# S5 in stages between the weight chunks, its parameters on GpSimd, and partition moves by TensorE products, in a hybrid decoder trunk

## The chip, the cores and the metric

The kernel runs on one core of a Trainium2 chip. The core has five engines with queues of their own: TensorE (PE in the profile; PEld is its weight load), VectorE (DVE), ScalarE (ACT), GpSimd (POOL) and SyncE (SP), and DMA queues that SyncE and ScalarE issue. The metric is the device time of one execution in microseconds; less is better.

## The reference, cut to what matters

Two layers (DEPTH = 2) of width 1024 over T = 272 tokens, in float32. A layer projects the normed input once, feeds four token mixers from it, merges them by gates and ends with an MLP of width 4096.

```python
proj = u @ w_in[l]
(rq, rk, rv, rg, s5u, sz, sxbc, sdt, hq, hf, hi, hgate, gates) = jnp.split(proj, split_at, axis=-1)
y_ret = retention_mixer(rq, rk, rv, rg, ret_gn_w[l])
y_s5 = s5_mixer(s5u, ...)
y_ssd = ssd_mixer(sz, sxbc, sdt, ...)
y_hg = hgrn2_mixer(hq, hf, hi, hgate, lb_all[l], hgrn_norm_w[l])
...
mixed = jnp.sum(gate * proj_b, axis=2) @ w_out[l]
h = h + rms_norm(mixed, norm_post_mix[l])
```

The mixer that is rearranged is S5: 32 groups of 16 channels, with 64 complex states each.

```python
mag = jnp.exp(lr * step)
ab_re, ab_im = mag * jnp.cos(li * step), mag * jnp.sin(li * step)
...
bu_re = jnp.einsum('btgj,gpj->btgp', uf, bb_re)      # and bu_im
_, _, xr, xi = lax.associative_scan(combine, (a_re, a_im, bu_re, bu_im), axis=1)
y = einsum(xr, c_re) - einsum(xi, c_im) + d_skip * u
y = jax.nn.gelu(y)
a, gt = jnp.split(y @ glu_w + glu_b, 2, axis=-1)
return a * jax.nn.sigmoid(gt)
```

Retention turns its queries and keys by a rotary embedding: with x1 and x2 the two halves of 32 channels in a head, `[x1*cos - x2*sin, x1*sin + x2*cos]`.

## The kernel before

**Weights.** All weights come as 336 chunks of 128 x 1024 floats in a fixed order (`ORDER`), 168 a layer. `chunk` (L307) loads one by SyncE's queue into one of three buffers (`wst`); ScalarE rounds it to a high half (`whi`, L325, three buffers), VectorE subtracts that for a low half (`wlo`, L327, two buffers). `gemm` (L331) makes of each block of 128 columns three products with one-pass operands: high by high (L344), high by the activation's low half (L345), low by high (L347). A chunk has 24 such products into a bank `g`, of which there are three. Chunks of a layer, numbered from its start: 0 to 11 HGRN's inputs, 12 to 19 SSD's, 20 to 23 S5's input, 24 to 27 HGRN's gate, 28 to 35 merge gates, 36 to 39 SSD's gate, 40 to 43 HGRN's branch, 44 to 51 merge gates, 52 to 59 retention's queries (52, 53), keys and values, 60 to 63 SSD's branch, 64 to 67 retention's gate, 68 to 83 merge gates, 84 to 87 the GLU of S5, 88 to 95 two branches, then the output projection and the MLP. Products that aren't weight chunks (attention, S5, transposes) are in plain float32 and are recorded as two matmuls each.

**Order.** The program is written as one stream; a planner builds each engine's instruction list ahead of time from it, by priority in the order of the text and by a modelled time at which operands are ready. `high_priority(offset)` moves instructions ahead; `issue_after(x)` puts them behind `x` on its engine. Each engine runs its list strictly in that order.

**S5.** `s5_params` (L833) makes, once for both layers, powers, exponentials and tables from three parameter columns; nearly 200 instructions on VectorE, on 128 x 32 elements mostly. Each layer handles its 16 column groups in four batches. `s5_prep` loads the batch's B and C values by ScalarE's queue into `s5a` and makes from them, on VectorE (three outer products of 128 x 512, three instructions each) and on GpSimd (one, and a table of six instructions, L987 to L992), the operands; `kd` and `bt` are its small products on TensorE. `s5_run` multiplies the input (L1109), scans the states with VectorE and GpSimd, and multiplies out (L1143, L1146). `s5_out` applies GELU to two batches and moves 32-partition blocks to other partitions by 16 copies (L1160 VectorE, L1162 ScalarE). All buffers of a batch (`s5a` to `s5g`) exist once. All four batches stand in the text behind `s5_in`; layer 1's first prepare stands in layer 0 behind `ssd_fin`.

**Rotary.** `ret_in` multiplies a 32-partition half by the sine table into the other half's partitions on GpSimd (L1496, four instructions of 32 x 1088), the whole by the cosine table, and adds.

The functions that the change touches, with their line numbers:

Of the kernel before, what the change touches and what calls it, by code (L numbers as in the profile page):

```python
# [13 lines left out]
ALU = mybir.AluOpType  # L14
# [57 lines left out]
for _name, _w in (("ident", 128), ("ones", 128), ("cen", 128), ("m432", 432), ("he", 1), ("ho", 1), ("le", 1), ("lo", 1),  # L72
                  ("rh", 1), ("rl", 1), ("r1", 1)):
    CONSTS[_name] = (_n, _w)
    _n += _w
# [12 lines left out]
AK, WARM = 5, 14  # L88
LH, LO, LU = (2,), (2,), (2,)
# [4 lines left out]
def shape_constants():  # L94
# [10 lines left out]
    put("cen", np.eye(128) - 1.0 / 128)  # L105
    t = np.arange(T)
# [27 lines left out]
    for i in range(2):  # L134
        for q in range(4):
# [3 lines left out]
            for k in range(2):  # L139
# [3 lines left out]
                sgn = 1.0 if q % 2 == 0 else -1.0  # L143
# [90 lines left out]
class Net:  # L234
    def __init__(self, ctx, tc, io, dbg=None):
# [24 lines left out]
        self.hold = {}  # L260

# [71 lines left out]
    def gemm(self, out, w, wk, x, xk, n, start=True, stop=True, after=None, late=False):  # L333
# [72 lines left out]
    def layer(self, l):  # L406
# [45 lines left out]
        s5y = self.s5(l, self.s5_in(l, u_all))  # L452
# [7 lines left out]
        if not last:  # L460

            idle, self.ahead = self.s5_prep(l + 1, 0)
# [7 lines left out]
        s5y = self.glu(l, s5y, (8, 2), sl)  # L470
# [362 lines left out]
    def s5_params(self):  # L833

        nc = self.nc
        v = nc.vector
# [7 lines left out]
        def tt(o, a, b, op):  # L844
            v.tensor_tensor(out=o, in0=a, in1=b, op=op)

        def ts(o, a, s1, op0, s2=None, op1=None):
            if op1 is None:
                v.tensor_scalar(out=o, in0=a, scalar1=s1, scalar2=None, op0=op0)
            else:  # L850
                v.tensor_scalar(out=o, in0=a, scalar1=s1, scalar2=s2, op0=op0, op1=op1)
# [26 lines left out]
        v.scalar_tensor_tensor(out=cs, in0=z, scalar=-0.5, in1=cs, op0=ALU.mult, op1=ALU.add)  # L878
# [5 lines left out]
        v.scalar_tensor_tensor(out=q, in0=q, scalar=-4.0, in1=k, op0=ALU.mult, op1=ALU.add)  # L884
# [23 lines left out]
        v.memset(pw[:, 0, 0], 1.0)  # L908
        v.memset(pw[:, 1, 0], 0.0)
# [13 lines left out]
        cmul(*P(3), *P(2), *P(1))  # L923
        cmul(*P(4), *P(2), *P(2))
# [18 lines left out]
        for s in (2, 1, 0):  # L943
            cmul(c5[:, 0, s], c5[:, 1, s], cR, cI, *P(3 - s))
# [607 lines left out]
```

## Time and profile before

| | us |
|---|---|
| median of 3 runs | 1277.0 (1274.56 to 1277.59) |
| the profiled execution | 1277.68 |
| its span, first to last instruction | 1275.9 |
| TensorE busy | 1216.1 |
| VectorE busy | 893.0 |
| ScalarE busy | 694.2 |
| GpSimd busy | 411.0 |

The profile is of one execution. Busy time of an engine is the union of its instructions' records; matmul records overlap, since a matmul starts while the one before it drains, so a busy TensorE is not one at its peak. The waits view lists idle time of an engine and what released it. A row by stretch gives the stretch in us from the span's start, its length, then the busy us of PE, PEld, DVE, ACT and POOL with their instructions (x), the granted clock, the share of the DMA engines and GB/s. Granted clock is that of TensorE, 1.00 for 2.4 GHz and 0.50 for 1.2 GHz.

### The profile page before, as it was taken

The numbers are of one execution on the slowest core, as the hardware profiler recorded it, in microseconds if no ns is written. First come the engines' busy times: TensorE is split into PE (matmuls) and PEld (weight loads), VectorE is DVE, ScalarE is ACT, GpSimd is POOL, SyncE is SP. The second block draws the span as 40 slices with busy tenths as digits, with TensorE's granted clock in tenths as the row PEclk, the third lists the DMA queues.
The fourth block names the chain that finished last, engine by engine and source line by source line (L and its number), as shares of the span: only waits on it lengthen the run. The fifth ranks groups of instructions, "written<-read, shape, count | busy, mean of one in ns | idle before, by whom it ended". The sixth has DMA issues, their size and how long they took to land.

```text
span 1275.9 us, 24312 instructions
## 1 busy us (share of the span) xinstructions
PE 1216.1 (95%) x9534; PEld 1174.6 (92%) x9534; DVE 893.0 (70%) x1480; ACT 694.2 (54%) x1219; POOL 411.0 (32%) x422
## 2 busy tenths in 40 slices
PE   8999998879999989999989999988999998999997
PEld 7999897879999989999979998987999998999996
DVE  8999989885637675544468995898656487655444
ACT  7446746443745665544455558354647546665442
POOL 2452467668002142200024333575170031322001
PEclk9999999989999989999989999998999998999998
DMA  6423232344354535555434332333444553555552
GB/s 238 160 98 104 101 123 99 108 136 145 135 175 173 176 110 178 173 175 178 170 108 143 126 123 97 123 111 114 146 150 149 184 179 136 169 188 189 182 184 98
DMA packets 53187, 186.69 MB, mean 146 GB/s; under 512 B 6096, under 2 KB 7248, under 8 KB 53072
## 3 DMA queue, kind: packets, MB, share of 16 engines
q1 hardware_dynamic: 50480, 179.40, 41.2%
q10 hardware_dynamic: 2592, 5.74, 1.4%
q8 instruction: 75, 1.23, 0.4%
q14 instruction: 40, 0.33, 0.1%
HBM read 184.06 MB, written 1.05 MB: 145 GB/s over the span
## 4 chain that ended last, share of the span: by engine, by line
PE 76%; DVE 13%; issue 4%; POOL 3%; ACT 2%; DMA 1%; SPq 0%; DVEq 0%; ACTq 0%; POOLq 0%
PE g L347 22%; PE g L344 22%; PE g L345 22%; DVE wlo L327 3%; PE mb L726 1%; PE ma L1263 1%; PE mb L717 1%; POOL S L1496 1%; DVE h L604 1%; DMA s5a<-in_bc 1%; DVE big_npom L601 1%; DVE s5a L1012 1%; ACT whi L325 1%; PE ma L726 1%; PE mb L1109 1%
## 5 line engine op out<-in xcount | busy, mean ns | idle before, releaser
L327 DVE TENSOR_TENSOR wlo<-wst,whi 128x1024 fp32r<-128x1024 f32 x336 | 438.5, 1306 | 259.1 <-PE g L347 220.8
L325 ACT ACTIVATE whi<-wst 128x1024 fp32r<-128x1024 f32 x336 | 355.8, 1060 | 365.3 <-PE g L345 287.6
L347 PE MATMUL g<-xh_u,wlo 128*128 128x272 f32 (+1 forms) x1024 | 299.7, 294 | 16.0 <-DVE wlo L327 15.8
L344 PE MATMUL g<-xh_u,whi 128*128 128x272 f32 (+1 forms) x1024 | 299.5, 293 | 0.6 <-ACT early L1068 0.4
L345 PE MATMUL g<-xl_u,whi 128*128 128x272 f32 (+1 forms) x1024 | 297.8, 291 | 0.0
L344 PE MATMUL g<-S,whi 128*128 128x272 f32 (+1 forms) x832 | 236.0, 288 | 4.6 <-ACT S L541 4.1
L347 PE MATMUL g<-S,wlo 128*128 128x272 f32 (+1 forms) x808 | 230.0, 288 | 1.7 <-DVE wlo L327 1.7
L345 PE MATMUL g<-S,whi 128*128 128x272 f32 (+1 forms) x768 | 220.4, 289 | 2.2 <-DVE S L552 1.9
L347 PEld LDWEIGHTS g<-xh_u,wlo 128*128 128x128 f32 x1024 | 195.7, 192 | 21.0 <-DVE wlo L327 18.2
L344 PEld LDWEIGHTS g<-xh_u,whi 128*128 128x128 f32 x1024 | 196.5, 192 | 2.6 <-ACT early L1068 0.7
L345 PEld LDWEIGHTS g<-xl_u,whi 128*128 128x128 f32 x1024 | 196.5, 192 | 1.5 <-issue 1.2
L344 PEld LDWEIGHTS g<-S,whi 128*128 128x128 f32 x832 | 157.1, 190 | 5.3 <-ACT S L541 4.5
L347 PEld LDWEIGHTS g<-S,wlo 128*128 128x128 f32 x808 | 151.9, 189 | 2.6 <-DVE wlo L327 2.2
L345 PEld LDWEIGHTS g<-S,whi 128*128 128x128 f32 x768 | 145.8, 190 | 4.1 <-DVE S L552 4.0
L345 PE MATMUL g<-xl_npm,whi 128*128 128x272 f32 (+1 forms) x512 | 147.7, 291 | 1.2 <-DVE xl_npm L552 1.2
L344 PE MATMUL g<-xh_npm,whi 128*128 128x272 f32 (+1 forms) x512 | 143.6, 289 | 2.4 <-ACT xh_npm L541 2.4
L347 PE MATMUL g<-xh_npm,wlo 128*128 128x272 f32 (+1 forms) x496 | 140.5, 288 | 0.0
L345 PEld LDWEIGHTS g<-xl_npm,whi 128*128 128x128 f32 x512 | 99.1, 193 | 1.9 <-DVE xl_npm L552 1.7
L344 PEld LDWEIGHTS g<-xh_npm,whi 128*128 128x128 f32 x512 | 96.7, 193 | 2.9 <-ACT xh_npm L541 2.9
L677 POOL TENSOR_TENSOR acc<-acc,tmp 128x272 f32<-128x272 f32 (+1 forms) x48 | 38.9, 828 | 186.0 <-DVE tmp L676 186.0
L347 PEld LDWEIGHTS g<-xh_npm,wlo 128*128 128x128 f32 x496 | 94.2, 192 | 0.2
L507 POOL TENSOR_TENSOR tmp<-tmp 128x272 f32<-128x272 f32 (+1 forms) x64 | 45.7, 714 | 137.3 <-DVE wlo L327 79.5
(377 smaller groups left out, 2184.4 us busy)
## 6 DMA issues: line engine op xcount, KB each, us to landing
wst<-in_w SPq DMA_DIRECT2D x336, 512.0 KB, 3.5
S<-in_rot ACTq DMA_DIRECT2D x4, 544.0 KB, 6.8
s5a<-in_bc ACTq DMA_DIRECT2D x8, 256.0 KB, 3.4
h<-in_h SPq DMA_DIRECT2D x4, 272.0 KB, 5.5
S<-in_ssdc ACTq DMA_DIRECT2D x2, 384.0 KB, 4.4
dtc<-in_ssdc ACTq DMA_DIRECT2D x2, 272.0 KB, 4.7
out<-h SPq DMA_DIRECT2D x2, 256.0 KB, 2.8
S<-in_lvl SPq DMA_DIRECT2D x1, 448.0 KB, 7.2
```

The lines of the kernel that those rows point to most:

```text
L325: a = nc.scalar.activation(hi, st, AF.Copy)
L327: nc.vector.tensor_tensor(out=lo, in0=st, in1=hi.bitcast(F32), op=ALU.subtract)
L344: self.nc.tensor.matmul(out, lhsT=a, rhs=r, start=st, stop=False)
L345: self.nc.tensor.matmul(out, lhsT=a, rhs=s, start=False, stop=False)
L347: end = self.nc.tensor.matmul(out, lhsT=b, rhs=r, start=False, stop=en)
L507: nc.gpsimd.tensor_tensor(out=q, in0=a, in1=a, op=ALU.mult)
L601: e.tensor_tensor(out=mw[:, k], in0=mw[:, k], in1=r, op=ALU.mult)
L604: e.tensor_tensor(out=self.h[:, k, sl], in0=self.h[:, k, sl], in1=mw[:, k], op=ALU.add)
L677: nc.gpsimd.tensor_tensor(out=a, in0=a, in1=t, op=ALU.add)
L717: nc.tensor.matmul(ps[:, c0:c0 + T - q0], lhsT=k[b, 128 * s:128 * s + 128], rhs=q[b, q0:T], start=True, stop=True)
L726: nc.tensor.matmul(out[:, t:T], lhsT=v01[s] if s < 2 else v2, rhs=P[:, p0:p0 + T - t], start=s == 0, stop=s == 2)
L1012: e.tensor_tensor(out=tmp, in0=X[1 - r], in1=F[1], op=ALU.mult)
```

## The change

S5's four batches are cut into four steps each (prepare, products, states, outputs), and `chunk` starts a step when the chunk count reaches the step's place: batch b's steps at chunks 24 + 10 b + 0, 3, 5 and 8 of the layer. Their first matmuls are put behind the last product of the chunk before. `s5_end` finishes ahead of the GLU. `s5_params` runs on GpSimd, where three-operand instructions become two and some complex products are joined. The partition moves of `s5_out` become products with 32 columns of the identity, 32 in a call, two calls a layer; ScalarE copies or splits their banks. Retention's halves are exchanged by a product with a permutation (`swap`), four a layer, followed by a VectorE and two GpSimd instructions each. The prepare of layer 1's first batch stands behind the GLU. The squares of retention are in slot 4 and not 11.

```diff
+S5_AT = (0, 3, 5, 8), 10
...
+    put("swap", np.eye(128)[p ^ 32])
...
     def chunk(self, *want):
         nc = self.nc
         assert ORDER[self.wi] == want, (ORDER[self.wi], want)
+        while self.stages and self.stages[0][0] <= self.wi:
+            self.stages.pop(0)[1]()
...
+        self.last = end
         return end
...
         if l == 0:
             self.s5_params()
-        s5y = self.s5(l, self.s5_in(l, u_all))
+        self.s5(l, self.s5_in(l, u_all))
...
-        if not last:
-
-            idle, self.ahead = self.s5_prep(l + 1, 0)
...
-        s5y = self.glu(l, s5y, (8, 2), sl)
+        assert not self.stages
+        s5y = self.glu(l, self.s5_end(), (8, 2), sl)
+        if not last:
+
+            idle, self.ahead = self.s5_prep(l + 1, 0)
...
         def tt(o, a, b, op):
-            v.tensor_tensor(out=o, in0=a, in1=b, op=op)
+            g.tensor_tensor(out=o, in0=a, in1=b, op=op)
...
-        v.scalar_tensor_tensor(out=r, in0=k, scalar=-PIO2[0], in1=th, op0=ALU.mult, op1=ALU.add)
-        v.scalar_tensor_tensor(out=r, in0=k, scalar=-PIO2[1], in1=r, op0=ALU.mult, op1=ALU.add)
-        v.scalar_tensor_tensor(out=r, in0=k, scalar=-PIO2[2], in1=r, op0=ALU.mult, op1=ALU.add)
+        for i, c in enumerate(PIO2):
+            ts(z, k, -c, ALU.mult)
+            tt(r, z, r if i else th, ALU.add)
...
-        for s in (2, 1, 0):
-            cmul(c5[:, 0, s], c5[:, 1, s], cR, cI, *P(3 - s))
+        sh = [128, 3, DEPTH, 16]
+        d = d4[:, 0:96].rearrange("p (i l q) -> p i l q", i=3, l=DEPTH)
+        cmul(c5[:, 0, 0:3], c5[:, 1, 0:3], *[pw[:, r, 3:0:-1] for r in range(2)],
+             *[x.unsqueeze(1).to_broadcast(sh) for x in (cR, cI)])
...
     def s5(self, l, W):
-        yf = self.slot(6, [128, 4, 68, 4])
+
+        nc = self.nc
+        yf = self.slot(6, [128, 2, 68, 4])
+        Y = self.cmy[:, 2:4].rearrange("p a (q c) -> p (a q) c", q=4)
+        now = {}
+
+        def prep(b):
+            if l and b == 0:
+                now["fs"], now["prep"] = (), self.ahead
+            else:
+                now["fs"], now["prep"] = self.s5_prep(l, b, self.decay if l and b == 1 else self.begin)
+
+        def products(b):
+            for f in now["fs"]:
+                f(self.tc.issue_after(self.last.ins))
+
+        def states(b):
+            now["run"] = self.s5_run(l, b, W, now["prep"], Y[:, 4 * (b % 2):4 * (b % 2) + 4])
+            next(now["run"])
+
+        def outputs(b):
+            next(now["run"])
+            if b == 1:
+                for i, ps in enumerate(self.s5_out(Y)):
+                    nc.scalar.activation(yf[:, i], ps, AF.Copy)
+
+        def end():
+            gh, gl = self.slot(9, [128, 4, T], F32R), self.slot(7, [128, 4, T], F32R)
+            cs = lambda a: a.rearrange("p (c s) -> p c s", s=4)
+            for i in range(2):
+                self.split(yf[:, i], cs(gh[:, i]), cs(gl[:, i]))
+            for i, ps in enumerate(self.s5_out(Y)):
+                self.split(ps, cs(gh[:, 2 + i]), cs(gl[:, 2 + i]))
+            return gh, gl
+
+        self.s5_end = end
         for b in range(4):
...
+            for at, f in zip(S5_AT[0], (prep, products, states, outputs)):
+                self.stages.append((self.wi + b * S5_AT[1] + at, lambda f=f, b=b: f(b)))
...
-        for q in range(4):
+        out = []
+        for a in range(2):
+            ps = self.bank("mb")[:, :T].rearrange("p (s c) -> p s c", s=4)
             for s in range(4):
-                o, i = yf[32 * q:32 * q + 32, b:b + 2, :, s], G[32 * s:32 * s + 32, :, q, :]
-                if q % 2:
-                    nc.vector.tensor_copy(o, i)
-                else:
-                    nc.scalar.activation(o, i, AF.Copy)
+                for q in range(4):
+                    nc.tensor.matmul(ps[32 * q:32 * q + 32, s], lhsT=self.c("ident")[:, 32 * s:32 * s + 32],
+                                     rhs=G[:, a, q], start=True, stop=True)
+            out.append(ps.rearrange("p s c -> p c s"))
+        return out
...
-        for q in range(4):
-            a, b = slice(32 * q, 32 * q + 32), slice(32 * (q ^ 1), 32 * (q ^ 1) + 32)
-            g.tensor_tensor(out=sw[b], in0=qk[a], in1=rot[1][a], op=ALU.mult)
-        g.tensor_tensor(out=qk, in0=qk, in1=rot[0], op=ALU.mult)
         qf, k = self.slot(14, [128, 4, T]), self.kpad[1]
         q = qf[:, 0:2]
-        g.tensor_tensor(out=q, in0=qk[:, 0:2], in1=sw[:, 0:2], op=ALU.add)
-        g.tensor_tensor(out=k[:, :, 0:T], in0=qk[:, 2:4], in1=sw[:, 2:4], op=ALU.add)
+        for i in range(4):
+
+            ps = self.bank()[:, :T]
+            nc.tensor.matmul(ps, lhsT=self.c("swap"), rhs=qk[:, i], start=True, stop=True)
+            nc.vector.tensor_tensor(out=sw[:, i], in0=ps, in1=rot[1][:, i], op=ALU.mult)
+            g.tensor_tensor(out=qk[:, i], in0=qk[:, i], in1=rot[0][:, i], op=ALU.mult)
+            g.tensor_tensor(out=q[:, i] if i < 2 else k[:, i - 2, 0:T], in0=qk[:, i], in1=sw[:, i], op=ALU.add)
...
-        sq, r = self.slot(11, [128, 4, T]), self.slot(1, [128, 4, T])
+        sq, r = self.slot(4, [128, 4, T]), self.slot(1, [128, 4, T])
```

## Rows read from the trace of the kernel before

**Rows 1.** The page: busy time of each engine, and a group of products

```profile
...
PE 1216.1 (95%) x9534; PEld 1174.6 (92%) x9534; DVE 893.0 (70%) x1480; ACT 694.2 (54%) x1219; POOL 411.0 (32%) x422
...
L347 PE MATMUL g<-xh_u,wlo 128*128 128x272 f32 (+1 forms) x1024 | 299.7, 294 | 16.0 <-DVE wlo L327 15.8
...
```

**Rows 2.** Busy time by stretch (x instructions), clock, DMA share, GB/s

```profile
...
160.00:290.00 130.00, 113.85 (x860) 108.20 (x861) 111.78 (x155) 64.43 (x121) 86.25 (x90) 0.96 0.35 117
290.00:334.00 44.00, 44.00 (x333) 41.30 (x333) 24.72 (x30) 20.48 (x41) 22.75 (x14) 1.00 0.38 131
334.00:418.00 84.00, 84.00 (x668) 83.92 (x667) 49.93 (x65) 46.02 (x72) 10.43 (x14) 1.00 0.50 170
761.00:811.00 50.00, 49.83 (x374) 44.32 (x374) 33.51 (x50) 36.98 (x74) 12.83 (x9) 1.00 0.32 111
811.00:910.00 99.00, 87.04 (x665) 82.57 (x664) 84.87 (x126) 51.77 (x96) 62.66 (x68) 0.93 0.33 108
...
```

**Rows 3.** TensorE's waits, 160 to 290 us: us in total, times, longest

```profile
...
PE g L347 <- DVE wlo L327: 9.5, 4, 2.9
PE g L344 <- DVE acc L673: 3.8, 2, 3.0
PE mc L1043 <- POOL s5c L1013: 1.3, 1, 1.3
...
```

**Rows 4.** TensorE's waits, 811 to 910 us

```profile
...
PE g L347 <- DVE wlo L327: 4.9, 3, 1.9
PE g L344 <- DVE acc L673: 3.2, 2, 2.6
PE mb L1109 <- DVE S L1148: 2.4, 2, 1.7
PE mc L1043 <- POOL s5c L1013: 0.9, 1, 0.9
...
```

**Rows 5.** Busy time by stretch, two stretches; PEclk is the granted clock

```profile
...
230.70:234.10 3.40, 3.40 (x18) 3.40 (x17) 3.40 (x8) 0.48 (x1) 0.13 (x1) 0.50 0.37 149
...
278.50:285.30 6.80, 6.09 (x27) 6.09 (x28) 3.13 (x5) 2.17 (x5) 0.22 (x1) 0.50 0.69 239
...
```

**Rows 6.** TensorE's waits, 761 to 811 us

```profile
...
PE ma L1292 <- issue: 0.2, 1, 0.2
```

**Rows 7.** Groups on VectorE, 112 to 334 us: busy us, mean ns, idle before

```profile
...
L1012 DVE TENSOR_TENSOR s5a<-s5a,s5c 128x512 f32<-128x512 f32 x10 | 8.6, 856 | 6.5 <-DMA s5a<-in_bc 6.4
...
L1160 DVE COPY S<-S 32x136 f32<-32x136 f32 x16 | 4.8, 303 | 0.2
...
L1115 DVE TENSOR_TENSOR S<-mb,s5e 128x272 f32<-128x272 f32 x4 | 1.7, 433 | 0.0
...
```

**Rows 8.** Busy time by stretch, columns as in rows 2

```profile
...
112.00:164.00 52.00, 50.87 (x376) 46.02 (x375) 49.91 (x140) 39.75 (x80) 22.27 (x16) 1.00 0.34 116
32.00:112.00 80.00, 78.79 (x646) 75.29 (x645) 79.87 (x241) 38.39 (x71) 36.22 (x32) 1.00 0.36 124
...
```

**Rows 9.** Busy time by stretch of L845 alone (S5 parameters, VectorE)

```profile
...
112.00:164.00 52.00, 16.77 (x87) 1.00 0.34 116
...
```

**Rows 10.** Busy time by stretch of L1255 alone (64-column weights): PE, PEld

```profile
...
103.30:104.10 0.80, 0.68 (x8) 0.54 (x8) 1.00 0.59 97
...
```

**Rows 11.** Busy time by stretch of L726 alone (attention): PE, PEld

```profile
...
117.70:119.54 1.84, 1.77 (x12) 1.68 (x12) 1.00 0.00 0
138.55:139.60 1.05, 0.98 (x10) 0.82 (x10) 1.00 0.68 176
...
```

**Rows 12.** TensorE's waits, 112 to 160 us

```profile
...
PE g L347 <- DVE wlo L327: 1.1, 1, 1.1
```

**Rows 13.** Groups on GpSimd by form, 20 to 112 us

```profile
...
L1237 POOL TENSOR_TENSOR S<-S 128x32 f32<-128x32 f32 x1 | 0.2, 240 | 0.1
...
```

**Rows 14.** Line L987: duration ns min/median/max, first and last start

```profile
...
L987 POOL TENSOR_TENSOR s5e<-s5ea,s5eb x8: 683/936/1533, 149.7 to 871.5; 128x288 f32<-128x288 f32 x8
...
```

**Rows 15.** Line L327: duration ns min/median/max, first and last start

```profile
...
L327 DVE TENSOR_TENSOR wlo<-wst,whi x336: 1192/1225/3474, 6.0 to 1258.6; 128x1024 fp32r<-128x1024 f32 x168
...
```

More of the change, by code (lines that the diff above doesn't have):

```diff
@@ L71 @@
 _n = 0
-for _name, _w in (("ident", 128), ("ones", 128), ("cen", 128), ("m432", 432), ("he", 1), ("ho", 1), ("le", 1), ("lo", 1),
+for _name, _w in (("ident", 128), ("ones", 128), ("cen", 128), ("swap", 128), ("m432", 432), ("he", 1), ("ho", 1), ("le", 1), ("lo", 1),
                   ("rh", 1), ("rl", 1), ("r1", 1)):
@@ L260, in __init__ @@
         self.hold = {}
+        self.stages = []
+        self.last = None
     def slot(self, k, shape, dt=F32):
@@ L877, in s5_params @@
         tt(cs, cs, z, ALU.mult)
-        v.scalar_tensor_tensor(out=cs, in0=z, scalar=-0.5, in1=cs, op0=ALU.mult, op1=ALU.add)
+        ts(z, z, -0.5, ALU.mult)
+        tt(cs, cs, z, ALU.add)
         ts(cs, cs, 1.0, ALU.add)
@@ L883, in s5_params @@
         ts(q, q, MAGIC, ALU.subtract)
-        v.scalar_tensor_tensor(out=q, in0=q, scalar=-4.0, in1=k, op0=ALU.mult, op1=ALU.add)
+        ts(q, q, -4.0, ALU.mult)
+        tt(q, q, k, ALU.add)
         tt(d, q, q, ALU.mult)
@@ L922, in s5_params @@
         cmul(*P(2), *P(1), *P(1))
-        cmul(*P(3), *P(2), *P(1))
-        cmul(*P(4), *P(2), *P(2))
+        sh = [128, 2, DEPTH, 16]
+        d = d4[:, 0:64].rearrange("p (i l q) -> p i l q", i=2, l=DEPTH)
+        cmul(pw[:, 0, 3:5], pw[:, 1, 3:5], pw[:, 0, 1:3], pw[:, 1, 1:3],
+             *[x.unsqueeze(1).to_broadcast(sh) for x in P(2)])
         c5 = self.cp.tile([128, 2, 4, DEPTH, 16], F32, name="s5c")
@@ L1080, in s5 @@
     def s5(self, l, W):
-        yf = self.slot(6, [128, 4, 68, 4])
-        for b in range(4):
-            Y = self.cmy[:, 2:4].rearrange("p a (q c) -> p (a q) c", q=4)
-            if l and b == 0:
-                prep = self.ahead
-            else:
-                fs, prep = self.s5_prep(l, b, self.decay if l and b == 1 else self.begin)
-                for f in fs:
-                    f()
-            self.s5_run(l, b, W, prep, Y[:, 4 * (b % 2):4 * (b % 2) + 4])
-            if b % 2:
-                self.s5_out(b - 1, Y, yf)
-        yf = yf.rearrange("p a c s -> p a (c s)")
-        gh, gl = self.slot(9, [128, 4, T], F32R), self.slot(7, [128, 4, T], F32R)
-        for i in range(4):
-            self.split(yf[:, i], gh[:, i], gl[:, i])
-        return gh, gl
+        nc = self.nc
[27 more added lines that the diff above has]
+        self.s5_end = end
+        for b in range(4):
+            for at, f in zip(S5_AT[0], (prep, products, states, outputs)):
+                self.stages.append((self.wi + b * S5_AT[1] + at, lambda f=f, b=b: f(b)))
     def s5_run(self, l, b, W, prep, Y):
@@ L1108, in s5_run @@
             for q in range(4):
-                nc.tensor.matmul(vp[:, q], lhsT=bi[:, r, q], rhs=W[:, 4 * b + q], start=True, stop=True)
+                with self.tc.issue_after(self.last.ins):
+                    nc.tensor.matmul(vp[:, q], lhsT=bi[:, r, q], rhs=W[:, 4 * b + q], start=True, stop=True)
             V.append(vp)
@@ L1140, in s5_run @@
                         op=ALU.mult)
+        yield
         yp = self.bank("mb")[:, :T].rearrange("p (q c) -> p q c", q=4)
         for q in range(4):
-            nc.tensor.matmul(yp[:, q], lhsT=ki[:, q].rearrange("p s x -> p (s x)"), rhs=W[:, 4 * b + q],
-                             start=True, stop=False)
+            with self.tc.issue_after(self.last.ins):
+                nc.tensor.matmul(yp[:, q], lhsT=ki[:, q].rearrange("p s x -> p (s x)"), rhs=W[:, 4 * b + q],
+                                 start=True, stop=False)
             for r in range(2):
@@ L1148, in s5_run, with s5_out @@
         v.tensor_tensor(out=Y, in0=yp, in1=du, op=ALU.add)
-    def s5_out(self, b, Y, yf):
+        yield
+    def s5_out(self, Y):
         nc = self.nc
```

18 lines of the change are left out of this document (9 added, 9 removed).

## The prediction

> **What bounds the kernel now.** I read the page first. TensorE is busy 95% of the span [rows 1], and in a stretch that nothing disturbs it starts 668 records in 84.0 us, one each 126 ns [rows 2]; a weight chunk of 24 such products is then 3.0 us. So every added product lengthens the kernel, and only stalls of TensorE can be won back. The view of TensorE's waits, taken by stretch, says where they are: while layer 0 works on S5 (160 to 290 us) 9.5 + 3.8 + 1.3 = 14.6 us [rows 3], while layer 1 does (811 to 910 us) 4.9 + 3.2 + 2.4 + 0.9 = 11.4 us [rows 4]. Nearly all are for VectorE: the low half of a weight chunk, or a gated sum that frees a bank.
>
> The waits have a second price. In the granted-clock column of the view by stretch, five stretches inside the S5 parts stand at 0.50 (1.2 GHz instead of 2.4), each behind waits: two of 6.8 us, three of 3.4 us; one of each is shown [rows 5]. The short one holds 18 records where 3.4 us at 126 ns would hold 27, so 1.1 us are lost; the long one holds 27 instead of 54, 3.4 us, of which some 0.7 us is a wait counted above. Together 3 x 1.1 + 2 x 2.7 = 8.7 us. There is a third price: a record lasts 294 ns but its successor starts after 126 [rows 1, 2], so each of the 20 waits in rows 3 and 4 hides 0.17 us more, 3.4 us. What S5's crowding costs is 14.6 + 11.4 + 8.7 + 3.4 = 38 us.
>
> Why VectorE is late is seen in its busy share by stretch [rows 2]: 111.8 of 130 us and 84.9 of 99 us, 86% in both S5 parts; 67% in the stretch ahead of layer 1's, where TensorE waits 0.2 us in all [rows 6], and 59% and 56% behind layer 0's, where it is busy throughout. Besides, VectorE sat 6.5 us for the S5 operands' DMA [rows 7], with weight splits queued behind.
>
> **The change part by part.**
>
> *Stages.* A batch's prepare, products, states and outputs are tied to chunks 24 to 62 of a layer, ten chunks apart; now they are wherever the planner finds room, crowded into the two parts above. No S5 operation goes away: the same work is thinned. VectorE in layer 0 from 112 to 290 us works 49.9 + 111.8 - 4 (overlap) = 158 us [rows 2, 8]; minus the parameters (16.8 us there [rows 9]), minus the copies (4.8 us [rows 7]), plus four rotary products of 0.43 us (as multiplications that read a bank now [rows 7]), that is 138; with 10 us for the 18 us up to 308, 148 of about 190 us, 78%. Layer 1 in the same way: 33.5 + 84.9 + 19 (as behind layer 0's part) - 3 = 134 of about 178 us, 75%. That lies midway between the 67% that brings no wait and the 86% that brings 38 us. Waits grow faster than load, and a load ten chunks ahead also hides the DMA; I take 70% of the 38 us as won, 27 us. The bounds are nothing and 38.
>
> *S5's outputs by TensorE.* Two calls a layer of 32 products with 32-column weights and 68 columns: 128 products, each two records, 256. The trace has none of this shape. Nearest are weights and columns of 64: eight records in 0.68 us [rows 10], without the last one's 0.17 us tail 0.064 each; so 256 x 0.064 = 16.4 us if they run one after another. They go to four column groups in turn. The trace has two groups: two heads' attention into two 64-row halves takes 0.98 us, against 1.77 us for the same columns at full width [rows 11] (two of its twelve records are missing), 0.55. With two groups' gain this is 9.0 us; with twice that for four, 4.5. I take 9, the nearer, and keep 4.5 to 16.4. The Trainium skill ("TensorE: Matmul & The Clock Gate", Part 3, Packing small matmuls) says that tiles in different column groups run side by side, and gives 2.38 times the speed for three of them; the trace agrees that two overlap, 1.8 times. By that rule this term would be about 6.9 us, an estimate from 16.4.
>
> *Rotary by TensorE.* Eight products of 272 columns, sixteen records; the full-width records take 1.77 us for 1728 columns [rows 11], 1.02 ns each: 16 x 272 x 1.02 = 4.4 us. It removes GpSimd multiplications on 32 partitions that no row of TensorE's waits names, so it buys nothing directly. A bank is now released by a VectorE product that needs the sine table, loaded behind the first query chunk, and the value turns queue behind on the same two banks. I take nothing (a chunk's matmuls can go first); at most one chunk, 3 us, a layer.
>
> *Parameters on GpSimd.* VectorE loses 16.8 us from 112 to 164 us [rows 9] and somewhat less before; that is worth little, since TensorE waits 1.1 us for weight splits there [rows 12]; I credit 1. GpSimd gains some 178 small instructions (191 now, minus 18 by joined complex products, plus 5 by splits). At their size, 32 elements, one takes 240 ns [rows 13]: 43 us. GpSimd is free 80 - 36 + 52 - 22 = 74 us from 32 to 164 us [rows 8], so at this price they end at about 120 us, earlier than today, where VectorE does 16.8 us of them after 112, and nothing waits. The upper price is the first rival.
>
> *Costed at nothing.* Layer 1's first prepare, with its DMA on ScalarE's queue, goes behind the GLU: VectorE is 59%, ScalarE 55% and GpSimd 12% busy there [rows 2]; a high half queues behind that DMA, and were the cover gone, nine VectorE products would cost up to one chunk, 3 us, once. The outputs' splits have until chunk 84 where the GLU begins; stages end at 62. Retention's squares in another buffer hold back gates four chunks later at the earliest.
>
> **Sum.** The profiled execution took 1277.7 us (span 1275.9), 0.7 over the median of the runs. 1277.7 - 27 - 1 + 9 + 4.4 = 1263. The own range of this case is 1250 to 1273.
>
> **Rivals.**
>
> *The parameters come late on GpSimd (slower).* TensorE's order is fixed when the program is built; if the first batch's products stand in it for parameters at 120 us and these come later, TensorE stands still. GpSimd's durations aren't steady: one and the same 288-element product takes 683 to 1533 ns [rows 14], 2.2 times. What it shares with VectorE speaks for this: weight splits take 1192 ns at best and 3474 at worst [rows 15], and VectorE is busy 79.9 of 80 us from 32 to 112 [rows 8]. At 2.2 x 240 = 540 ns the 178 take 96 us, 53 more, and end near 190. TensorE would not stand that long, for then VectorE runs out of weight splits and leaves GpSimd its 240 ns: with 60 to 100 instructions left, 14 to 24 us, plus 10 for the prepare. That gives 1287 to 1297. It decides from 14 us of stall, where the gain is gone: 0.08 us per instruction above what the order assumes. Against it: TensorE waits for GpSimd's large S5 products only 1.3 and 0.9 us today [rows 3, 4], so the order knows these; and a batch may slip to chunk 84. Chance 0.2. The Trainium skill ("SBUF — State Buffer", Who interferes with whom) says that a VectorE instruction with two SBUF inputs and a GpSimd instruction that reads SBUF exclude each other for an instruction's length; the spread in the rows agrees, and by that rule this rival is the likelier.
>
> *The waits stay (slower).* A prepare still queues nine VectorE products around the weight splits, and thinning may only move the jams. With 20% won: 1277.7 - 8 + 13.4 = 1283, range 1274 to 1291. For it: the chunks onto which batch 0 is spread are full already, 49.9 of 52 us [rows 8]. Against: copies, parameters and a fifth prepare leave the part. Chance 0.18.
>
> *All waits go and four groups overlap fully.* 1277.7 - 39 + 4.5 + 4.4 = 1248, from 1244 to 1250. Chance 0.09.
>
> *Gain and added products cancel*: half of 38 won, the outputs at 13: 1277.7 - 19 + 17.4 = 1276. Chance 0.08.
>
> **How the numbers follow.** The forecast has 0.45. About 0.3%, 3.8 us, is what can be told from no change here. Faster (under 1273): 0.45 + 0.09 + 0.03 of the rivals' lower ends, 0.57. Same: 0.08 + 0.05 of the first two rivals, 0.13. Slower: their rest, 0.30. The range goes down to 1247, within the best case, and up to 1291, which leaves out the upper half of the first rival alone.
>
> **What would show it.** Right: TensorE's waits for weight splits in the S5 parts drop to a third; the five stretches at 0.50 become none or one; VectorE's share there is under 80%; 256 new output records add 4 to 16 us, rotary ones 4. Wrong: TensorE waiting over 10 us for S5's first batch between 120 and 170 us, with small GpSimd instructions above 0.5 us; or VectorE still near 86%, with waits of 25 us.

## The result: slower by 1.4%, and the profile after

After the change the median is 1294.56 us (1291.93 to 1296.98, 4 runs) against 1276.66 us (4 runs): a ratio of 1.0136, 95% interval 1.0114 to 1.0159. The forecast was 1263, the range 1247 to 1291. The sign is wrong and the time lies outside the range.

The page of the changed kernel, busy time first, then three of the rows in 40 slices of 32.3 us:

```profile
PE 1224.7 (95%) x9806; PEld 1180.3 (91%) x9806; DVE 849.2 (66%) x1266; ACT 683.1 (53%) x1192; POOL 429.6 (33%) x601
...
PE   8975999999999989999989999989999998999997
...
POOL 3999215555500332110015242464730031321001
PEclk9997899999999999999999999999999999999998
```

TensorE has 272 records more than in [rows 1]: the 256 of the outputs and the 16 of the rotary swap, as counted. VectorE works 44 us less, GpSimd only 19 us more, so the sums look harmless. The slices tell otherwise. In the second to fourth, 32 to 129 us, GpSimd is at 9 while TensorE falls to 7 and 5. That is HGRN in layer 0, a part that the change does not mention. By stretch, the first two answering to [rows 8], the third to [rows 2]:

```profile
32.00:112.00 80.00, 65.28 (x493) 61.99 (x493) 62.03 (x118) 28.34 (x49) 78.12 (x176) 0.94 0.31 102
112.00:164.00 52.00, 42.71 (x285) 38.70 (x284) 30.28 (x54) 25.95 (x61) 25.40 (x41) 0.84 0.18 60
160.00:290.00 130.00, 125.70 (x1044) 120.78 (x1043) 98.57 (x141) 75.20 (x131) 58.70 (x65) 1.00 0.39 131
```

From 32 to 112 us GpSimd is busy 78.12 of 80 us (36.22 before), and VectorE, which was full at 79.87, is *idle* for 18 us. The engine that was relieved of work stands still: its longest wait there, 6.1 us, is for ScalarE's L1398, which itself waits for GpSimd (below). In layer 0's S5 part, 160 to 290 us, VectorE's share is 76% and the clock full: there the change does what was hoped.

To say where time went I compare the starts of the same product of the weight chunks (the first of each chunk's eight high-by-high products) in the traces; a chunk holds the same work in every kernel, wherever it stands in time. The numbers are differences of two starts, in us:

| chunks | before | after | difference |
|---|---|---|---|
| 8 to 24 (HGRN's levels, SSD's and S5's inputs, layer 0) | 75.9 | 123.7 | +47.8 |
| 24 to 84 (S5's stages, layer 0) | 269.7 | 242.2 | -27.5 |
| 192 to 252 (the same in layer 1) | 251.4 | 246.9 | -4.5 |
| all else in the span | 678.9 | 678.6 | -0.3 |

The 27.5 us are not all a gain: while HGRN stood still, the engines did SSD's and S5's first work ahead of these chunks, so that TensorE starts 1948 products in this range, 99 fewer than with the parameters back on VectorE (first experiment). There the same range is 266.6, 3.1 under before.

What TensorE waited for in the whole kernel, largest groups of the changed one:

```profile
PE g L353 <- DVE wlo L333: 7.1, 10, 2.0
PE ma L1306 <- POOL S L1367: 7.0, 3, 3.7
...
PE ma L1306 <- DVE S L1313: 3.8, 1, 3.8
...
PE ma L1298 <- POOL S L1367: 3.7, 1, 3.7
...
PE ma L1298 <- DVE S L1369: 2.6, 1, 2.6
```

L1306 and L1298 are HGRN's level products (L1263 and above it before), L1367 its level multiply on GpSimd, L1369 its twin on VectorE. The waits for weight splits, which took 9.5 us in one of the S5 parts alone [rows 3], are down to 7.1 in all, and new ones stand in HGRN. GpSimd's parameter instructions: the busy time of L853, which issues most of them, from 32 to 112 us, then their ns as least, median and most, and who waited for them:

```profile
32.00:112.00 80.00, 48.46 (x129) 0.94 0.31 102
...
L853 POOL TENSOR_TENSOR s5b<-s5b x73: 231/253/1231, 3.7 to 115.8; 128x32 f32<-128x32 f32 x73
...
L853 POOL TENSOR_TENSOR s5eb<-s5eb,s5c x6: 401/689/1435, 85.0 to 100.9; 128x32 f32<-128x32 f32 x2, 128x64 f32<-128x64 f32 x2, 128x128 f32<-128x128 f32 x2
...
  ACT s5b L1044: 8.5, 1
  ACT L1398: 7.4, 1
  DVE s5b L1026: 5.6, 1
  PEld ma L1306: 2.7, 2
```

L1044 and L1026 prepare S5's first batch. L1398 belongs to SSD's step sizes and needs no parameter: ahead of it ScalarE issues two loads (L280) that wait for one-column copies on GpSimd (L278), and these stood behind parameter instructions until 67 us. GpSimd's timeline shows the queue (start, us, line, and how many in a row):

```profile
90.82 0.91 POOL L1367 TENSOR_TENSOR S<-S,S 128x272 f32<-128x272 f32 x1
91.69 0.30 POOL L853 TENSOR_TENSOR s5c<-s5eb,s5b 128x64 f32<-128x64 f32 x1
...
95.49 1.30 POOL L853 TENSOR_TENSOR s5eb<-s5eb,s5c 128x64 f32<-128x64 f32 x1
...
100.02 0.89 POOL L1367 TENSOR_TENSOR S<-S,S 128x272 f32<-128x272 f32 x1
```

Between two level multiplies GpSimd runs parameter instructions for 8.3 us, back to back. TensorE's timeline has the answer: its level products at 100.97 us waited 3.66 us for the second of them.

```profile
100.97 1.16 PE L1306 MATMUL ma<-S,S 128*128 128x128 f32 x8 [3.66 <-POOL S L1367]
```

The clock then falls too (the last four entries of a row by stretch are GpSimd's busy time with its instructions, the granted clock, the DMA share and GB/s):

```profile
60.00:80.00 20.00, 16.08 (x119) 15.44 (x117) 13.10 (x22) 7.06 (x13) 19.76 (x59) 0.91 0.32 108
80.00:100.00 20.00, 13.62 (x109) 12.27 (x109) 20.00 (x41) 7.16 (x12) 19.92 (x35) 1.00 0.25 85
100.00:120.00 20.00, 15.11 (x96) 14.32 (x96) 12.48 (x23) 2.55 (x5) 19.84 (x50) 0.83 0.15 53
120.00:140.00 20.00, 13.09 (x75) 11.72 (x76) 18.89 (x40) 8.14 (x24) 13.16 (x16) 0.66 0.12 40
...
122.50:136.10 13.60, 9.19 (x45) 7.90 (x46) 13.46 (x29) 4.83 (x15) 9.83 (x12) 0.50 0.18 59
```

The granted clock of 0.83 and 0.66 is an average over stretches at 1.2 and at 2.4 GHz; those at 1.2, of which the last row is one, stand behind waits. Of the five half-clock stretches of the S5 parts [rows 5], one of 3.4 us is left, in layer 1; HGRN has five new ones, the longest of 13.6 us.

### The profile page after: what moved, and what is told of

It is laid out like the page before. It is cut to its first block, busy times and chain, and to the rows that moved or that the text cites. A ratio compares the mean times of both kernels' runs of the same rounds, so it can differ in the third digit from the quotient of the medians.

```text
span 1291.3 us, 24754 instructions
## 1 busy us (share of the span) xinstructions
PE 1224.7 (95%) x9806; PEld 1180.3 (91%) x9806; DVE 849.2 (66%) x1266; ACT 683.1 (53%) x1192; POOL 429.6 (33%) x601
## 4 chain that ended last, share of the span: by engine, by line
PE 74%; DVE 11%; POOL 9%; issue 2%; ACT 2%; DMA 2%; SPq 0%; DVEq 0%; ACTq 0%; POOLq 0%
PE g L350 22%; PE g L353 21%; PE g L351 21%; DVE wlo L333 2%; POOL s5b L853 2%; PE mb L734 1%; POOL s5c L853 1%; PE mb L1147 1%; PE mb L725 1%; DMA s5a<-in_bc 1%; DVE h L612 1%; PE mb L1186 1%; DVE xl_npm L560 1%; POOL s5eb L853 1%; POOL S L1367 1%
## 5 line engine op out<-in xcount | busy, mean ns | idle before, releaser
L333 DVE TENSOR_TENSOR wlo<-wst,whi 128x1024 fp32r<-128x1024 f32 x336 | 430.0, 1281 | 246.0 <-PE g L353 195.2
L685 POOL TENSOR_TENSOR acc<-acc,tmp 128x272 f32<-128x272 f32 (+1 forms) x48 | 41.7, 886 | 188.4 <-DVE tmp L684 188.3
L515 POOL TENSOR_TENSOR tmp<-tmp 128x272 f32<-128x272 f32 (+1 forms) x64 | 42.6, 666 | 140.1 <-DVE wlo L333 96.8
## 6 DMA issues: line engine op xcount, KB each, us to landing
s5a<-in_bc ACTq DMA_DIRECT2D x8, 256.0 KB, 3.4
out<-h SPq DMA_DIRECT2D x2, 256.0 KB, 2.8
```

The lines of the kernel that those rows point to most:

```text
L333: nc.vector.tensor_tensor(out=lo, in0=st, in1=hi.bitcast(F32), op=ALU.subtract)
L515: nc.gpsimd.tensor_tensor(out=q, in0=a, in1=a, op=ALU.mult)
L685: nc.gpsimd.tensor_tensor(out=a, in0=a, in1=t, op=ALU.add)
```

## The experiments

Fifteen kernels ran, each beside before. Medians and ratios to before:

| kernel | us | ratio, 95% interval | chunks 8-24 | 24-84 | 192-252 |
|---|---|---|---|---|---|
| 1 parameters on VectorE | 1271.76 | 0.9951 (0.9936 to 0.9966) | 76.6 | 266.6 | 246.7 |
| 2 parameters on GpSimd alone | 1315.24 | 1.0289 (1.0272 to 1.0306) | 126.0 | 258.5 | 251.7 |
| 3 parameters behind the levels | 1280.22 | 1.0017 (1.0004 to 1.0029) | 76.8 | 274.2 | 247.9 |
| 4 as 1, rotary as before | 1272.76 | 0.9958 (0.9941 to 0.9974) | 76.1 | 272.2 | 244.0 |
| 5 parameters split | 1288.27 | 1.0093 (1.0071 to 1.0114) | 102.4 | 258.5 | 246.8 |
| 6 stages alone | 1277.63 | 1.0002 (0.9990 to 1.0014) | 77.7 | 275.5 | 245.2 |
| 7 as 1, outputs in a block | 1270.05 | 0.9941 (0.9924 to 0.9957) | 75.9 | 267.5 | 245.0 |
| 8 as 1, 14 chunks apart | 1259.67 | 0.9864 (0.9845 to 0.9882) | 75.9 | 257.0 | 243.9 |
| 9 level multiply on VectorE | 1293.09 | 1.0128 (1.0114 to 1.0142) | 107.1 | 257.8 | 248.9 |
| 10 as 7, 14 chunks apart | 1254.03 | 0.9820 (0.9807 to 0.9834) | 75.9 | 254.4 | 241.3 |
| 11 as 1, 17 chunks apart | 1261.08 | 0.9876 (0.9861 to 0.9890) | 76.5 | 256.0 | 244.3 |
| 12 as 6, 14 chunks apart | 1267.63 | 0.9932 (0.9918 to 0.9946) | 76.7 | 264.7 | 246.3 |
| 13 first batch behind the levels | 1288.43 | 1.0087 (1.0065 to 1.0109) | 92.1 | 269.6 | 247.3 |
| 14 as 13, loads' copies on VectorE | 1289.62 | 1.0095 (1.0076 to 1.0113) | 94.3 | 266.4 | 247.6 |
| 15 as 14, level multiply on VectorE | 1282.47 | 1.0050 (1.0031 to 1.0069) | 94.0 | 258.4 | 247.6 |

### 1 and 2: the parameters alone

In 1 the changed kernel gets back the old `s5_params`; in 2 the old kernel gets the new one.

```diff
     def s5_params(self):
-        v, g = nc.vector, nc.gpsimd
+        v = nc.vector
...
-            g.tensor_tensor(out=o, in0=a, in1=b, op=op)
+            v.tensor_tensor(out=o, in0=a, in1=b, op=op)
```

> The changed kernel with s5_params back on VectorE, as it was; stages, outputs and rotary stay changed. Theory Q (the parameters' small GpSimd instructions stand in GpSimd's queue between HGRN's level updates, and TensorE waits for these from 40 to 140 us): the loss there goes, the gain in the S5 parts stays: 1255 to 1268 us. Rival S (the stages, the output products or the rotary products are what costs): 1285 to 1300 us.

> The kernel before with only s5_params taken over from the changed one (GpSimd); batches, outputs and rotary as before. Theory Q: all of the loss and none of the gain: 1300 to 1315 us. Rival S: 1273 to 1282 us, since VectorE has less to do and GpSimd is free.

Undoing the parameters takes 22.8 us off (1294.6 to 1271.8) and chunks 8 to 24 fall back to 76.6. Doing them alone adds 37 us and brings the like, 126.0. The 14 us between the two lie mostly in chunks 24 to 84: with the stages these win 24.4 us back (266.6 to 242.2), with the old order 11.2. So the whole loss is the parameters', and all else in the change gains 6 us. That is less than expected: 1271.8 is over the theory's range, as 1315.2 just is in the second run.

### 3: the parameters behind the levels

```diff
-            self.s5_params()
+            with self.tc.issue_after(self.up.ins):      # the last hgrn_up of layer 0
+                self.s5_params()
```

> The changed kernel with the parameters still on GpSimd, but all of them issued behind the last level update of HGRN in layer 0. Theory Q: HGRN's waits go although GpSimd does the same work: 1258 to 1275 us; it may lose some us where SSD's products on GpSimd now stand among the parameters. Rival P (GpSimd's small instructions slow VectorE and each other by the SBUF port they share, wherever they stand): over 1280 us, the waits move behind HGRN.

The same GpSimd instructions, later in GpSimd's order, cost 8.5 us instead of 22.8, and chunks 8 to 24 are whole again (76.8): place counts, not amount alone. The whole, 1280.2, is over what the theory of the queue allowed and on the bound of rival P, so the time alone does not refute that rival. TensorE's waits in kernel 3 from 130 to 200 us name whom the parameters hold now, S5's first batch and SSD's GpSimd product (L1486):

```profile
PE mc L1058 <- DVE s5b L1029: 5.4, 1, 5.4
PE mb L735 <- POOL S L1486: 3.5, 2, 2.6
```

### 5: the parameters cut in two

```diff
+        e = [g]                          # tt and ts now use e[0]
...
+        e[0] = v
         pw = self.cp.tile([128, 2, 5, DEPTH, 16], F32, name="s5p")
```

> The changed kernel, with the parameters of S5 cut in two: the reduction, the sines and cosines and what leads to them stay on GpSimd, from the powers on they go back to VectorE. Theory Q (GpSimd works its list in order, and HGRN's level updates stand behind parameter instructions in that list): the first part is issued before the levels begin, so little of it stands ahead of them: 1269 to 1275 us, at most 3 us over the version with all parameters on VectorE (1271.8). Rival C (any parameter work on GpSimd costs by its amount, through memory shared with VectorE): about half of the 22.8 us stays, 1281 to 1286 us.

1288.3 is over the ranges of both theories: 16.5 of the 22.8 us stay. The cut is not at the middle: 47 instructions with 18.8 us stay on GpSimd, where the whole set took 67.5, and 124 go to VectorE. Yet in chunks 8 to 24 they cost 25.8 us, over half of the whole set's 47, so the loss does not go by the amount of GpSimd's work. It does not show the queue either, since the run brings a wait of its own; VectorE's waits name it:

```profile
DVE s5p L854 <- POOL s5b L854: 3.8, 1, 3.8
```

The second half, on VectorE, waits for the first until 59.3 us, with weight splits behind it, and is then worked off among the levels: VectorE has 9.46 of 20 us busy from 40 to 60 us and 20.00 in each of the next three stretches, 71 parameter instructions (13.3 us) among them. In the kernel before, 51 of them ran from 40 to 60 us and only 22 (5.9 us) in the 60 us behind. A chain cut between two engines was as late here as its slower half.

### 9, 13, 14, 15: taking the victims out of the queue, one at a time

In 9 HGRN's level multiply of layer 0 leaves GpSimd. In 13, parameters as changed, the preparation of S5's first batch is queued behind HGRN's levels on all three engines. In 14 the two one-column copies of L278 leave GpSimd as well; 15 is 14 with 9. In 9 `self.up` is the number of the layer; in 13 and 14 `up`, `upv` and `upa` are the last level's instructions on GpSimd, VectorE and ScalarE.

```diff
-        nc.gpsimd.tensor_tensor(out=k4[:, :, :, 0], in0=k4[:, :, :, 0], in1=br, op=ALU.mult)
+        e = nc.vector if self.up == 0 else nc.gpsimd
+        e.tensor_tensor(out=k4[:, :, :, 0], in0=k4[:, :, :, 0], in1=br, op=ALU.mult)
...
+                with ExitStack() as st:
+                    if l == 0 and b == 0:
+                        for i in (self.up, self.upv, self.upa):
+                            st.enter_context(self.tc.issue_after(i.ins))
...
-    def load_after(self, out, in_, dep):
+    def load_after(self, out, in_, dep, e=None):
-        self.nc.gpsimd.tensor_copy(
+        (e or self.nc.gpsimd).tensor_copy(
```

> The changed kernel, parameters on GpSimd as changed, but HGRN's level multiply of layer 0 runs on VectorE: the victim leaves the queue that the parameters hold. Theory Q (the 47.8 us that chunks 8 to 24 lost are level updates standing behind parameter instructions on GpSimd): these chunks come back from 123.6 us to under 95 us, and the whole to 1270 to 1284 us, since S5's first batch then waits for the parameters instead. Rival C (any parameter work on GpSimd slows the stretch by its amount, whoever stands in the queue): chunks 8 to 24 stay over 110 us and the whole at 1288 to 1300 us.

> The changed kernel with the parameters on GpSimd where they were, but the preparation of S5's first batch in layer 0 (its copies on ScalarE, its complex products on VectorE and GpSimd) is queued behind HGRN's last level on each engine. Theory H (work on ScalarE and VectorE that needs the late parameters stands ahead of HGRN's and SSD's work and holds it: 8.5 and 5.6 us in the waits): chunks 8 to 24 fall from 123.6 us to 95 to 108 us, the whole to 1278 to 1288. Theory Q (only GpSimd's own queue counts): chunks 8 to 24 stay above 115 us.

> The version before, and also the two one-column copies ahead of SSD's constant loads in layer 0 run on VectorE instead of GpSimd, where they stood behind parameter instructions until 67 us and ScalarE's loads waited 7.4 us for them. Theory H: a further 3 to 8 us off chunks 8 to 24. Rival: the next GpSimd step of SSD or HGRN takes their place and nothing changes.

> The version before, and HGRN's level multiply of layer 0 on VectorE as well: neither GpSimd's queue nor the two other queues then hold a level behind the parameters. Theories H and Q together: chunks 8 to 24 within 10 us of the 76.6 us with the parameters on VectorE, though GpSimd does all the parameter work meanwhile; the whole 1272 to 1284 us. Rival C (GpSimd's work slows the stretch by its amount): chunks 8 to 24 stay over 95 us.

9 gave back 16.6 us of the 47.8, not the 29 or more expected, and 1.5 us of the whole: my theory that only GpSimd's own queue counts fell. The waits of ScalarE in kernel 9, and behind them those of TensorE, from 36 to 165 us, show the other way the delay travels:

```profile
ACT s5b L1044 <- POOL s5c L853: 12.5, 1, 12.5
```

TensorE:

```profile
PE g L350 <- ACT S L1447: 9.8, 2, 8.9
```

L1044, a copy for S5's first batch, waits for the parameters; behind it on ScalarE stands L1447, which empties a bank of SSD's input products; behind that stands TensorE, 8.9 us. TensorE names ScalarE, ScalarE names GpSimd: a wait must be followed to its end.

13 confirms that holder: chunks 8 to 24 fall to 92.1. But chunks 24 to 84 rise from 242.2 to 269.6 (24 to 28 alone from 17.5 to 36.2), since the first batch is now late itself, and the whole gains only 6. In 14 the copies' wait is gone and nothing is won; the next GpSimd steps take its place. TensorE's waits in kernel 14, same stretch, name the level multiply:

```profile
PE ma L1310 <- POOL S L1371: 13.3, 5, 7.7
```

VectorE's name a scaling of SSD's:

```profile
DVE S L1428 <- POOL dtc L1413: 8.5, 1, 8.5
```

15 takes the level multiply away again and gains 7, but in chunks 24 to 84 (266.4 to 258.4) and not in 8 to 24. Of VectorE's waits in it the one for a GpSimd product of SSD's step sizes is now the longest:

```profile
DVE dts L1422 <- POOL dts L1421: 7.2, 1, 7.2
```

With three holders removed, 12.1 of the 22.8 us are back. Chunks 8 to 24 missed the 10 us that I had set, at 94.0, just under the rival's bound of 95, so 17.4 us of their 47 stay and the run does not decide between the two. What the last 10.7 us of the whole are made of is not settled: more holders of this kind are seen (SSD's steps, the late first batch), and the slowing of GpSimd beside VectorE, measured below, is in every one of these runs.

### 6, 8, 11, 12: what the stages are worth, and at which spacing

6 keeps of the change only the stages, with the moved first prepare of layer 1 and the squares' slot; 8 and 11 are 1, and 12 is 6, with one constant changed.

```diff
-S5_AT = (0, 3, 5, 8), 10
+S5_AT = (0, 3, 5, 8), 14        # 17 in 11
```

> Of the change the stages alone: parameters on VectorE, outputs moved by copies on ScalarE and VectorE, rotary halves on GpSimd. The prediction's own terms give 27 us less than before, about 1250 us. Theory T (the crowding of S5's parts was worth only some 10 us to the stages, and the added products cost what they save on the other engines): 1266 to 1274 us, within 4 us of the version that also has the output products (1272.8).

> The version with parameters on VectorE, its S5 batches 14 chunks apart instead of 10. If the stages still crowd VectorE where they stand, thinning them gives 3 to 6 us, 1266 to 1269 us. Rival: the waits that are left come from single chains (a product on GpSimd, a gated sum) and not from the density, 1270 to 1274 us.

> Parameters on VectorE, batches 17 chunks apart (10 gave 1271.8, 14 gave 1259.7 us). Theory D (the density of S5's work on VectorE between 176 and 222 us sets the loss): most of it is gone at 14, so a further 0 to 5 us, 1255 to 1260 us. Rival: at 14 the last stages already stand in chunks 68 to 84, which went from 51.8 to 60.6 us, and at 17 they crowd the retention and the gates there: 1262 to 1270 us.

> Of the change the stages alone (copies for the outputs, rotary halves on GpSimd, parameters on VectorE), batches 14 chunks apart instead of 10, at which it gave 1277.6 us. Theory D (the spacing decides, because at 10 VectorE is as full as before): 1262 to 1268 us, a gain of 10 to 15 us over 10 chunks. Rival: the output products are what makes the wide spacing pay, 1272 to 1278 us.

The stages alone are worth nothing at ten chunks (1.0002, above the ranges of both theories): layer 1 gains 6.2 us, layer 0 loses 5.8. The half-clock stretches stay too: kernel 6 has five in the S5 parts, 23.8 us together, just as before. TensorE's three largest waits in layer 0 from 160 to 420 us in kernel 6 are 19.0 us, no less than the 14.6 us of [rows 3], and for the same kinds of releaser:

```profile
PE g L350 <- DVE acc L681: 7.9, 3, 4.8
PE g L353 <- DVE wlo L333: 5.7, 2, 4.6
PE g L350 <- DVE tmp L684: 5.4, 1, 5.4
```

At 14 chunks they are worth 9.7 us (12), and with the other parts 18 (8), where the step from 10 to 14 gives 12, twice the 3 to 6 that I had expected. The view by stretch of kernel 1, at ten chunks, and that of kernel 8 show where:

```profile
176.00:222.00 46.00, 36.87 (x346) 34.99 (x344) 43.49 (x62) 22.11 (x39) 37.12 (x40) 1.00 0.27 88
222.00:300.00 78.00, 75.87 (x581) 72.61 (x581) 53.82 (x71) 33.88 (x64) 34.74 (x40) 0.98 0.45 143
```

Kernel 8, at 14:

```profile
176.00:222.00 46.00, 43.76 (x346) 42.47 (x345) 45.33 (x68) 23.98 (x43) 26.68 (x30) 1.00 0.39 125
222.00:300.00 78.00, 78.00 (x659) 74.82 (x658) 51.19 (x63) 34.82 (x67) 43.99 (x48) 1.00 0.44 147
```

VectorE is nearly full in the first stretch in both. But at ten chunks the complex products of the batches (L1019 to L1021) take 12.9 us of it in 13 instructions, GpSimd works 37 us beside them, VectorE gets 8 weight splits done, and TensorE is busy only 36.87 of 46 us. At 14 the products take 8.8 us in 11 instructions, GpSimd works 27 us, VectorE gets 12 splits done, and TensorE is busy 43.76. No run separates the fewer products from the quicker ones. Behind it, from 222 us, VectorE has room in both (54 and 51 of 78). The wait for sums (L681, 6.5 us in kernel 1) is gone in kernel 8. At 17 (11) chunks 36 to 44 gain another 1.2 us, but 60 to 68 take 42.0 instead of 37.6 and 84 to 96 39.3 instead of 36.8, where the GLU stands: 1261.1, between the ranges of both theories.

### 4, 7, 10: rotary, outputs, and the best version

4 is 1 with the rotary halves on GpSimd as before. In 7 the output products are given a priority that keeps each set of 64 records together; 10 joins this with 14 chunks.

```diff
+                  with self.tc.high_priority(offset=3000):
                     nc.tensor.matmul(ps[32 * q:32 * q + 32, s], ...
```

> Parameters on VectorE as in the first of these runs, and retention's halves exchanged on GpSimd again, as before the change. If the eight rotary products cost what the prediction took (4.4 us, nothing hidden): 4 us under the first run. If GpSimd, loaded with the last S5 batches, then holds back retention's scores: 0 to 15 us over it.

> The version with parameters on VectorE, and each set of 256 output products put into TensorE's order as one block instead of in up to seven visits between the chunks' products. If the visits cost what chunks 68 to 84 and their like in layer 1 lost (3.4 and 3.0 us), 1265 to 1269 us. Rival: the block only moves the wait to the products behind it, 1271 to 1274 us.

> Parameters on VectorE, batches 14 chunks apart, and the output products as blocks in TensorE's order. If the two gains add (12.1 and 1.7 us), 1256 to 1260 us; the block alone was within the spread, so 1260 +- 2 us is as likely.

The rotary swap by TensorE nets 1 us, within the uncertainty: it shortens chunks 24 to 84 by 5.6 us (52 to 60 alone from 44.3 to 39.3) and lengthens 192 to 252 by 2.7 and the rest of the span by 2. The outputs' products in TensorE's timeline of the changed kernel, the first set of layer 0:

```profile
243.89 1.15 PE L1202 MATMUL mb<-S,cst 128*32 128x68 f32 x64
```

Three of the seven visits of the second set:

```profile
354.43 0.33 PE L1202 MATMUL mb<-S,cst 128*32 128x68 f32 x8
...
357.65 0.66 PE L1202 MATMUL mb<-S,cst 128*32 128x68 f32 x26
...
361.70 0.32 PE L1202 MATMUL mb<-S,cst 128*32 128x68 f32 x6
```

64 records take 1.15 us in one go, but a visit of 6 takes 0.32; the four sets of the changed kernel take 7.9 us in 17 visits. At ten chunks the block's gain is not told apart from nothing (0.9941 against 0.9951, intervals overlap, and over the 1265 to 1269 that I expected); at 14 it is, 0.9820 against 0.9864, with chunks 68 to 84 and 236 to 252 3.0 and 2.8 us shorter. Kernel 10, 1254.03 us, beats both kernels and the time expected of it. The busy times of its page:

```profile
PE 1210.5 (97%) x9806; PEld 1172.4 (94%) x9806; DVE 874.0 (70%) x1456; ACT 681.3 (54%) x1192; POOL 382.8 (31%) x424
```

TensorE's waits in it in layer 0 from 160 to 420 us, all of them, in place of the 14.6 us of [rows 3]:

```profile
PE g L353 <- DVE wlo L333: 2.5, 3, 1.1
PE mc L1051 <- POOL s5c L1021: 0.4, 1, 0.4
```

## Why the prediction was wrong

The terms as measured, each from the ratios of two kernels that differ in that part (kernel 6; 4 less 6; 1 less 4; after less 1), times 1277 us:

| term | forecast | measured |
|---|---|---|
| stages | -27 | +0.3 |
| outputs by TensorE | +9 (4.5 to 16.4) | -5.6, net |
| rotary by TensorE | +4.4 | -0.9, net |
| parameters on GpSimd | -1 | +23.6 (22.8 by medians) |
| sum | -14.6 | +17.4 |

**The step that failed is in "Parameters on GpSimd": "nothing waits".** The time of their end was right, about 120 us forecast and 119.9 measured (the last L853), but by luck. The reckoning was of free time on GpSimd, 74 us for 43 us of work, and both halves were wrong. The work took 67.5 us (the three lines that issue it, summed by stretch to 164 us), 173 instructions of 0.39 us in the mean instead of 0.24. And free time is not what counts on an engine that works its list in order: HGRN's level multiplies, SSD's scalings and the copies ahead of two loads are each short, and waits of TensorE end at them, in part by way of ScalarE and VectorE. The prediction named nobody who stands behind the parameters in GpSimd's queue, though the rows of GpSimd's work from 32 to 112 us were there to be asked whose work it was. Kernel 3 shows it from the other side: the same work behind the levels leaves them untouched. Kernels 13 to 15 bring 12.1 of the 22.8 us back by moving single holders; how the rest divides stays open. The signs that the prediction had set for being right came all the same, since they look at the S5 parts alone: in layer 0 from 160 to 420 us TensorE waits 1.7 us for weight splits, one half-clock stretch is left, VectorE's share is 76%.

The rival "The parameters come late on GpSimd" had the sign and the time, 1287 to 1297, at a chance of 0.2. Its price per instruction, 0.54 us, was as far from the 0.39 measured as the forecast's 0.24. It had one victim right in kind, S5's first batch, which waited 8.5 and 5.6 us; but it placed the loss in TensorE's products of that batch between 120 and 170 us. It lies in HGRN, from 60 to 140 us, because other chains' work stands behind the parameters on GpSimd, and behind the batch's on ScalarE and VectorE. The test that I wrote, TensorE over 10 us behind S5's first batch, would have missed it.

GpSimd's durations go with what VectorE does beside them, as that rival supposed. L853 has 113 products of 128 x 32 in the trace of the changed kernel. The 53 with no VectorE instruction beside them take 251 ns in the mean and 277 at most, which is the forecast's price. Sorted by the VectorE instruction that covers most of each, the 16 beside one that reads a matmul bank take 249 ns, the 23 beside a tensor-tensor instruction with both operands in SBUF 687. The Trainium skill ("SBUF — State Buffer", Who interferes with whom) says that a VectorE instruction with two SBUF inputs and a GpSimd instruction that reads SBUF exclude each other; the trace agrees. VectorE loses less: the 16 weight splits of chunks 8 to 24 take 1349 ns in the mean, 1248 before. What share of the 22.8 us this slowing is, no run here separates.

**Stages: the term was mis-sized, and its mechanism shows only at a wider spacing.** At the spacing of the change none of the 38 us of stalls is won on balance. The step was the average: 148 of 190 us, 78%, "midway" between shares with and without waits. An average over 190 us hides that VectorE is nearly full for 46 of them. The half-clock stretches fell to one in the changed kernel, but with the parameters back on VectorE (1) there are three, and with the stages alone five again. TensorE's waits stayed until the batches were moved by four chunks: from 160 to 420 us they are 15.9 us before, 24.1 in kernel 6, 12.3 in kernel 12. At 14 chunks the stages alone give 9.7 us. Kernel 10, with the outputs and the swap, is 23 us under before while it carries 9 us of added products (4.6, below, and the forecast's 4.4): some 32 of the 38 us, if these products hide nowhere. By its own waits (2.9 us in layer 0, 5.3 in layer 1) and its one half-clock stretch it is some 26; both are estimates. What was predicted is the gain of thinning, and ten chunks apart did not thin the full stretch. The 38 us were a little high besides: rows 3 and 4 show 15 waits and their whole views 19, not 20. What was costed at nothing cost nothing: all else in the span is 678.8 us in kernel 6 and 678.9 before.

**Outputs.** For sets kept together the rows' bound for four groups was the right one: 256 records x 1.15/64 us are 4.6 us, at the low end of 4.5 to 16.4 (the prediction took the value of two groups, 9). As they ran in the changed kernel, in visits, they took 7.9. The Trainium skill ("TensorE: Matmul & The Clock Gate", Part 3, Packing small matmuls) says that tiles in different column groups run side by side; the trace agrees, and the 4.6 us for four groups are under the 6.9 that the prediction estimated from its figure for three. What was not costed are the visits, up to 3 us a layer (kernels 7 and 10), and the gain. The copies that went were on the path: in kernel 6 eight of them stand in a row on VectorE from 312.7 us for 5.7 us, and TensorE waits 5.4 us for a sum (L684) behind them. Chunks 60 to 68 take 43.5 us with them (6) and 35.7 without (4), so that the net is below nothing.

**Rotary.** The products were costed at 4.4 us; their sixteen records are 5.2 us of TensorE's busy time in the trace, and no run prices them by themselves. That removing GpSimd's multiplications "buys nothing directly" was wrong by about as much, 5 us in chunks 52 to 60 of layer 0, but only beside the stages: before, with the same multiplications, these chunks take 39.1 us. In kernel 4 the multiplications run from 271.7 to 284.2 us, and VectorE's prepare products beside them take up to 3.0 us (L1021), 0.7 to 1.0 in the mean in kernels 1 and 8; TensorE waits 5.9 us for weight splits there.

## What to carry to other kernels

Before moving work to an engine with free time, list what else stands in its queue in that stretch and how soon each item is needed; a hundred short instructions in a row are one long one for whoever is behind them. Price the work for what the other engines do beside it: here a 128 x 32 product of 0.25 us became one of 0.37 in the mean. Then follow whoever waits for the moved work: on its own engine it holds others, and the profile names only the last link. When work is thinned by hand, the place and spacing are a size to be measured: 10, 14 and 17 chunks gave 1271.8, 1259.7 and 1261.1 us here.

## What the runs showed of the hardware that was not expected

- Four column groups of float32 products overlap nearly fully: 64 records of 68 columns in 1.15 us, 18 ns each, where records of 64 columns one after another take 64 ns each [rows 10]. A visit of 6 between other products took 0.32 us.
- A 128 x 32 product on GpSimd took 231 ns at best, 253 in the median and 1231 at worst; larger ones, up to 128 x 128, 689 in the median of one group. On VectorE the same kind of instruction took 171, 182 and 1144 ns in the kernel before.
- The same product on GpSimd took 251 ns with VectorE idle beside it, 249 beside a VectorE instruction that reads a matmul bank, and 687 in the mean beside a VectorE tensor-tensor instruction with both operands in SBUF (53, 16 and 23 records of the changed kernel).
- Four multiplications of 32 x 1088 on GpSimd (12.5 us) stretched a VectorE product of 128 x 512 beside them to 3.0 us (kernel 4), where its like takes 0.7 to 1.0 in the mean.
